# A decoder layer's seven-product weight pairs: an order of the units, the place of one weight sum, and two late additions

## The chip, the cores and the metric

The kernel runs as one program on one core of a Trainium2 chip. The metric is device time in microseconds, the median of several runs. A core has a matrix engine (TensorE, PE in the profile), VectorE (DVE), ScalarE (ACT), GpSimd (POOL) and SyncE (SP), each with its own in-order queue of instructions, and 16 DMA engines which they feed. Work of two engines is ordered only by semaphores: an instruction that waits holds back everything behind it on its engine.

## The reference

One decoder layer over 256 tokens of width 2048 in float32: retention and RG-LRU mixers side by side, a gated merge, cross-attention to 256 memory tokens, a convolutional gated FFN of width 5632, and a final norm. What matters here are three matrix products that end in a residual sum:

```
h = h + merged @ w_mix_out[l]
...
    return o @ w_o
...
    return (jax.nn.silu(gate) * val) @ w_down
```

## The kernel before

Almost all time goes into products with weights that are read once: `weight_plan` lists them, and `entry_units` (L117) cuts each into **units** of one megabyte, 4 blocks of 128 rows by 512 columns. Each unit is loaded to a tile `raw`, and then split in two float32r parts so that three fast products stand for one exact product: ScalarE rounds `raw` to `hi` (L281, "the cast"), VectorE makes `lo = raw - hi` (L282). TensorE then adds up activation-hi by weight-hi, activation-lo by weight-hi, and activation-hi by weight-lo.

`units` (L296) and `prefetch` (L241) run this as a stream. Ahead of the products of a unit, `prefetch` has written the load, the cast and the `lo` of the next two units (`AHEAD = 2`) into the program. There are five `raw` buffers, and three each for `hi` and `lo`: the cast of unit n takes the buffer of unit n-3, so it waits until TensorE is through with that unit. Loads are issued on SyncE in order, each waiting for a free `raw` buffer. `later(n, fn)` (L292) puts off a piece of work until n more units have been handed out. The order of instructions on each engine is in the end decided by a scheduler of the framework, which may pull single matmuls of a later unit ahead of the rest of an earlier one.

**Pairs.** Six times (once for `w_mix_out`, once for `xa_w_o`, and twice in each of the first two FFN parts) two neighbouring column blocks c0 and c1 of 512 are done together by `pair_add` (L364). Half of the contraction (k blocks 0 to 7) uses a seven-product scheme on 2x2 blocks: sums of the activations are made beforehand by `sums`, and sums of the weight blocks are made on the fly. The other half is done plainly. A pair is 11 units: seven "q" units of 12 matmuls each, and four "p" (plain) units of 24 matmuls. `PAIR_UNITS` (L98) is their order, written out by hand:

- q1 loads a block into a buffer that is kept, slot A. q3 loads a block into a second kept buffer, slot B.
- q2 is a plain load: column block c1 with the even k blocks; it multiplies plain activations.
- q5 uses A after a further block has been added to it. That addition is a DMA which accumulates (L260), issued on GpSimd. It must wait until the cast and the `lo` of q1 have read A.
- q6 uses A + B: `prefetch` makes that sum on VectorE (L262, 128 x 2048 elements) at the moment in which q6 is prepared, after q5's split has read A.
- q7 adds a block to B by accumulating DMA, after the sum has read B; q4 adds a block to A by accumulating DMA, after q6's split has read A.

The products of a pair go to three PSUM tiles of 128 x 1024: `xz` (halves x and z), `yv` (y and u), `rw` (r and w_). They are added to the two residual tiles h0 and h1 by VectorE (`add`, L383): x to h0 after q1, all of `rw` to h1 after q3, z twice to h1 after q5, x from h1 after q6, x to h0 and from h1 after q7, `yv` to h0 after q4. x is reused in between (q6 and q7 accumulate on), so q7's first product waits for q6's subtraction. In the program as built, 8 of the 24 matmuls of the third p stand ahead of q6's in all six pairs (the scheduler pulled them there), and in pairs 3 and 5 two of q5's stand near the beginning of the second p. Around the first pair, `memory_steps` has ScalarE square rows of `mem` (L882) between the casts.

Of the kernel before, what the change touches and what calls it, by code (L numbers as in the profile page):

```python
# [13 lines left out]
ALU = mybir.AluOpType  # L14
AX = mybir.AxisListType

P = 128
# [10 lines left out]
BW = 512  # L28
# [65 lines left out]
def residual_plan(w):  # L94
# [3 lines left out]
PAIR_UNITS = [  # L98
    ("q1", "A", ("new", 0, 0)),
    ("p", None, (1, 8)),  # L100
    ("q2", None, ("new", 1, 0)),
    ("p", None, (1, 12)),
    ("q3", "B", ("new", 1, 1)),
    ("q5", "A", ("add", 0, 1)),
    ("q6", "A", ("sum",)),
    ("p", None, (0, 8)),
    ("p", None, (0, 12)),
# [42 lines left out]
def hybrid_layer(  # L150
# [16 lines left out]
    act, dve, pe, pool, sp = nc.scalar, nc.vector, nc.tensor, nc.gpsimd, nc.sync  # L167
# [11 lines left out]
    def nm(s):  # L179
        count[0] += 1  # L180
        return f"{s}_{count[0]}"
# [7 lines left out]
    def acc():  # L189
        return pm.tile([P, 2, BW], F32, tag="acc", name=nm("acc"))  # L190
# [37 lines left out]
    held = {}  # L228
# [4 lines left out]
    def load_x(n):  # L233
        while len(xin) < n:
            t = big([P, 2, BW], s="nat")
            rows = x[0].rearrange("(t p) d -> p t d", p=P)
            c = len(xin) * BW
            act.dma_start(out=t, in_=rows[:, :, c : c + BW])
            xin.append(t)

    def prefetch(n):  # L241
        while len(ahead) < n and taken[0] < len(stream):
            kind, slot, op, i = stream[taken[0]]
            src = None if i is None else wall[i]
            taken[0] += 1
            first = taken[0] == 1
            if op == "new":
                raw = wp.tile([P, KC, BW], F32, tag="raw", bufs=RAW_BUFS, name=nm("raw"))
                if slot:
                    held[slot] = raw  # L250
            else:
                raw = held[slot]
            if taken[0] <= 4:
                xs.load(2 * taken[0] - 1)
            pieces = ((0, 1), (1, 2), (2, 4)) if first else ((0, 2), (2, 4)) if taken[0] <= 3 else ((0, 4),)
            for a, b in pieces:
                if op == "new":
                    sp.dma_start(out=raw[:, a:b, :], in_=src[:, a:b, :])
                elif op == "add":
                    pool.dma_start(out=raw, in_=src, accum_op=ALU.add)  # L260
                else:
                    dve.tensor_tensor(out=raw, in0=raw, in1=held["B"], op=ALU.add)  # L262
                if first and a == 0:
                    sp.dma_start(out=xs.rest[0], in_=xs.rest[1])
                elif first and a == 1 or a == 0 and taken[0] <= 4:
                    xs.load(2 * taken[0])
            if taken[0] == 5:
                sp.dma_start(out=cid, in_=consts[:, 0:C_DEC])
                sp.dma_start(out=pa[:, 16:P], in_=by_feature[:, 16:P])
                sp.dma_start(out=pb, in_=by_feature[:, P : P + 80])  # L270
            if taken[0] == 7:
                sp.dma_start(out=pf.rearrange("p a n -> p (a n)"), in_=by_feature[:, P + 80 :])
            hi = wp.tile([P, KC, BW], F32R, tag="hi", bufs=PART_BUFS, name=nm("hi"))
            lo = wp.tile([P, KC, BW], F32R, tag="lo", bufs=PART_BUFS, name=nm("lo"))
            for a, b in pieces:
                if taken[0] <= 4:
                    xs[2 * (taken[0] - 1) + (b - 1) // KH]
                if first and b <= KH:
                    dve.tensor_copy(hi[:, a:b], raw[:, a:b])  # L279
                else:  # L280
                    act.copy(hi[:, a:b], raw[:, a:b])  # L281
                dve.tensor_tensor(  # L282
                    out=lo[:, a:b], in0=raw[:, a:b], in1=hi[:, a:b].bitcast(F32), op=ALU.subtract
                )
            parts = [(hi[:, k : k + KH], lo[:, k : k + KH]) for k in range(0, KC, KH)]
            ahead.append((kind, parts))
            if taken[0] >= 4:
                load_x(min(4, 2 * (taken[0] - 3)))
# [3 lines left out]
    def later(n, fn):  # L292

        pending.append((step[0] + n + 1, fn))

    def units(*e):  # L296

        assert plan[gemms[0]] == e, (gemms[0], plan[gemms[0]], e)
        gemms[0] += 1
        for _ in entry_units(e):  # L300
            prefetch(1)
            kind, parts = ahead.pop(0)
            prefetch(AHEAD)
            yield kind, parts
            step[0] += 1
            due = [p for p in pending if p[0] <= step[0]]
            pending[:] = [p for p in pending if p[0] > step[0]]
            for _, fn in due:
                fn()
# [54 lines left out]
    def pair_add(w, row, st, ss, c0, c1, h0, h1):  # L364

        xz, yv, rw = acc(), acc(), acc()
        x, z, y, u, r, w_ = (t[:, i, :] for t in (xz, yv, rw) for i in range(2))
        where = {
            "q1": (x, "a", 0, 0), "q2": (y, "a", 1, 0), "q3": (r, "s", 3, 0), "q4": (u, "a", 1, 1),
            "q5": (z, "s", 0, 0), "q6": (x, "s", 1, 0), "q7": (x, "s", 2, 0),  # L370
        }
        begun, plain = set(), 0

        def run(o, key, ops, parts):
            for kk, (h, l) in enumerate(ops):
                hi, lo = (t[:, kk % KH, :] for t in parts[kk // KH])
                pe.matmul(o, h, hi, start=key not in begun, stop=False, skip_group_check=True)  # L377
                begun.add(key)
                pe.matmul(o, l, hi, start=False, stop=False, skip_group_check=True)  # L379
                pe.matmul(o, h, lo, start=False, stop=kk == KC - 1, skip_group_check=True)  # L380

        def add(o, i, op=ALU.add):
            dve.tensor_tensor(out=o, in0=o, in1=i, op=op)  # L383

        for kind, parts in units(w, row, NT, c0, c1):
            if kind == "p":
                k0, (a, b), (ka, kb) = ((8, (r, w_), "rw"), (12, (r, w_), "rw"), (8, (y, u), "yu"), (12, (y, u), "yu"))[plain]
                plain += 1
                for tt, (o, key) in enumerate(((a, ka), (b, kb))):
                    cs = slice(tt * P, (tt + 1) * P)  # L390
                    run(o, key, [halves(st[(k0 + k) // 2], k % 2, cs) for k in range(KC)], parts)
            else:
                o, t, j, tt = where[kind]
                if t == "a":
                    ops = [halves(st[k], j, slice(tt * P, (tt + 1) * P)) for k in range(KC)]
                else:
                    ops = [(ss[k][:, 0, j * P : (j + 1) * P], ss[k][:, 1, j * P : (j + 1) * P]) for k in range(KC)]
                key = {"q1": "x", "q4": "u", "q6": "x", "q7": "x", "q2": "y", "q3": "r", "q5": "z"}[kind]
                run(o, key, ops, parts)
            if kind == "q1":  # L400
                add(h0[:, 0, :], x)
            elif kind == "q3":
                add(h1, rw)
            elif kind == "q5":
                add(h1, z[:, None, :].to_broadcast([P, 2, BW]))
            elif kind == "q6":
                add(h1[:, 0, :], x, ALU.subtract)
            elif kind == "q7":
                add(h0[:, 1, :], x)
                add(h1[:, 1, :], x, ALU.subtract)  # L410
            elif kind == "q4":
                add(h0, yv)
# [27 lines left out]
    def halves(t, j, cs=slice(0, S)):  # L440

        return t[:, j, cs], t[:, j, S + cs.start : S + cs.stop]
# [12 lines left out]
    def joined(a, s="j"):  # L455

        c = tmp("c")
        o = tmp(s)
        with tc.high_priority(URGENT):
            act.copy(c, a[:, :, S:BW])  # L460
            dve.tensor_tensor(out=o, in0=a[:, :, 0:S], in1=c, op=ALU.add)  # L461
        return o
# [236 lines left out]
    for g in range(2):  # L699
        dec = big([P, 4, S], s="dec")  # L700
        vs, turned = [], []
        for b, o in enumerate((O_Q, O_K)):
            a = qjoin if g == b == 0 else [joined(t, "q") for t in gemm_t("w_in", 0, xs, NT, o + g * BW)]
            if b == 0:
                sp.dma_start(
                    out=dec,
# [245 lines left out]
    for b in range(XH):  # L952
        ks = []
        for a in gemm_t("xa_w_k", 0, ms, NT, b * BW):
            z = joined(a, "kz")
# [99 lines left out]
    for part, nb_ in enumerate(FF_PARTS):  # L1055
# [15 lines left out]
        if final:  # L1071
            wfin = []
            for i in range(2):
                t = big([P, 2, BW], s="wf")
                sp.dma_start(
                    out=t.rearrange("p a n -> p (a n)"),
# [3 lines left out]
        if nb_ == 4:  # L1080
            for b in (0, 2):
                pair_add("ffn_w_down", b0 * BW, hid, hid_sums, b * BW, (b + 1) * BW, hrow[b], hrow[b + 1])
        else:
            for b in range(4):
                down(b0, hid, b, final)
# [36 lines left out]
```

## Time and profile before

| what | value |
|---|---|
| median of 3 runs | 2067.07 us (2066.53 to 2070.82) |
| the profiled execution's own time | 2065.32 us |
| its span, first to last instruction | 2063.5 us |
| mean granted TensorE clock | 0.995 |
| HBM read | 401.04 MB, 195 GB/s over the span |
| starts of the six A + B sums (L262) | 852.4, 1237.2, 1512.1, 1556.3, 1781.5, 1825.7 us |

The profile page gives the busy time of each engine, the chain of work that ended last, and groups of instructions by source line. The trace behind it can be asked for a timeline of one engine, for the busy time and granted clock in chosen stretches ("windows"), for who waited for whom, and for the time from a DMA's issue to its landing. In a row of the timeline stand start, duration, engine, line, operation, tile written <- tiles read, and in brackets the idle time of the engine just before it with what ended that idle time. A matmul's duration there is its pipelined length; the distance of two starts is what counts. The six pairs lie at about 836 to 882, 1219 to 1267, 1493 to 1541, 1541 to 1585, 1763 to 1810 and 1811 to 1854 us. They are called pair 1 to pair 6 below. Pairs 3 and 4 follow each other without a gap, and so do 5 and 6.

### The profile page before, as it was taken

Reading aid. Unit: us, or ns where it says so; the run is one execution under the profiler, and the core shown is the slowest. Engines: PE = TensorE matmul, PEld = TensorE weight load, DVE = VectorE, ACT = ScalarE, POOL = GpSimd, SP = SyncE. Lnnn points to the kernel's source line nnn. Section 1 sums busy time; section 2 is a strip of 40 time slices with the busy share of each in tenths; the row PEclk is TensorE's granted clock in tenths of the full one; section 3 lists DMA queues with packets and bytes.
Section 4 is the critical chain, followed back from the end, with each engine's and each line's share of the span. In section 5 each row is a group of like instructions: output and inputs, shape, how many; then the busy total and the mean of one; then the engine's idle time right before and its main releaser. Section 6 shows DMA issues by size and latency. Waiting matters only on the chain.

```text
span 2063.5 us, 25096 instructions
## 1 busy us (share of the span) xinstructions
PE 2031.5 (98%) x10436; PEld 1735.4 (84%) x10436; DVE 1372.1 (66%) x1411; ACT 1039.6 (50%) x1042; POOL 23.7 (1%) x30
## 2 busy tenths in 40 slices
PE   9999999999999999999999999999999999999998
PEld 7888888888888888788888887888877888778887
DVE  6747658444688654666555656587786787776775
ACT  6445447433476544465444545555554555454543
POOL 0000000000000000000000000000000000000000
PEclk9999999999999999999999999999999999999999
DMA  9554553555553555865554447555567555675552
GB/s 371 208 206 163 184 194 143 204 186 202 198 199 143 201 187 184 265 238 211 182 184 164 163 163 224 184 188 183 193 194 263 186 190 195 183 245 204 185 203 82
DMA packets 66211, 404.76 MB, mean 196 GB/s; under 512 B 7217, under 2 KB 11953, under 8 KB 19377
## 3 DMA queue, kind: packets, MB, share of 16 engines
q1 hardware_dynamic: 61984, 381.66, 50.9%
q0 software_dynamic: 2592, 18.88, 4.9%
q10 hardware_dynamic: 1520, 2.63, 0.4%
q8 instruction: 81, 1.33, 0.2%
q14 instruction: 34, 0.27, 0.0%
HBM read 401.04 MB, written 2.10 MB: 195 GB/s over the span
## 4 chain that ended last, share of the span: by engine, by line
PE 91%; DVE 5%; ACT 2%; issue 1%; DMA 0%; SPq 0%; POOLq 0%; DVEq 0%; ACTq 0%
PE acc L339 43%; PE acc L349 12%; PE acc L351 12%; PE acc L350 12%; PE acc L380 3%; PE acc L377 3%; PE acc L379 3%; DVE lo L282 3%; PE sm L438 2%; ACT hi L281 1%; PE sm L450 1%; PE sm L764 0%; DVE raw L262 0%; DVE fv L998 0%; DMA raw<-in_wall 0%
## 5 line engine op out<-in xcount | busy, mean ns | idle before, releaser
L282 DVE TENSOR_TENSOR lo<-raw,hi 128x2048 fp32r<-128x2048 f32 (+2 forms) x378 | 855.8, 2267 | 531.2 <-ACT hi L281 530.7
L281 ACT CAST hi<-raw 128x2048 fp32r<-128x2048 f32 (+1 forms) x376 | 713.3, 1899 | 745.6 <-PE acc L350 291.9
L339 PE MATMUL acc<-s,hi 128*128 128x512 f32 x2688 | 638.8, 391 | 2.0 <-DVE hi L279 1.1
L339 PEld LDWEIGHTS acc<-s,hi 128*128 128x128 f32 x2688 | 496.4, 188 | 100.6 <-issue 2.2
L349 PE MATMUL acc<-hi,s 128*128 128x512 f32 (+1 forms) x1144 | 442.3, 387 | 0.0
L351 PE MATMUL acc<-lo,s 128*128 128x512 f32 (+1 forms) x1144 | 441.1, 386 | 0.0
L350 PE MATMUL acc<-hi,s 128*128 128x512 f32 (+1 forms) x1144 | 440.7, 385 | 0.0
L339 PEld LDWEIGHTS acc<-s,lo 128*128 128x128 f32 x2688 | 342.1, 191 | 12.7 <-DVE lo L282 1.9
L339 PE MATMUL acc<-s,lo 128*128 128x256 f32 x2688 | 349.6, 283 | 0.9 <-DVE lo L282 0.9
L351 PEld LDWEIGHTS acc<-lo,s 128*128 128x128 f32 x1144 | 215.0, 188 | 43.8 <-DVE lo L282 0.6
L349 PEld LDWEIGHTS acc<-hi,s 128*128 128x128 f32 x1144 | 215.1, 188 | 42.1 <-ACT s L471 0.3
L350 PEld LDWEIGHTS acc<-hi,s 128*128 128x128 f32 x1144 | 215.1, 188 | 41.9 <-DVE s L472 0.2
L380 PE MATMUL acc<-lo,s 128*128 128x512 f32 x264 | 105.5, 400 | 14.2 <-DVE lo L282 14.0
L377 PE MATMUL acc<-hi,s 128*128 128x512 f32 x264 | 105.1, 398 | 1.7 <-ACT hi L281 1.7
L379 PE MATMUL acc<-hi,s 128*128 128x512 f32 x264 | 105.1, 398 | 0.4 <-DVE s L472 0.4
L460 ACT COPY c<-acc 128x512 f32<-128x512 f32 x84 | 48.3, 579 | 99.1 <-PE acc L339 99.1
L380 PEld LDWEIGHTS acc<-lo,s 128*128 128x128 f32 x264 | 50.4, 191 | 27.8 <-DVE lo L282 17.7
L377 PEld LDWEIGHTS acc<-hi,s 128*128 128x128 f32 x264 | 50.6, 192 | 12.6 <-ACT hi L281 2.6
L379 PEld LDWEIGHTS acc<-hi,s 128*128 128x128 f32 x264 | 50.7, 192 | 11.9 <-DVE s L472 1.6
L383 DVE TENSOR_TENSOR nat<-nat,acc 128x512 f32<-128x512 f32 (+1 forms) x42 | 37.7, 910 | 20.0 <-PE acc L380 20.0
L461 DVE TENSOR_TENSOR uz<-acc,c 128x512 f32<-128x512 f32 x44 | 30.2, 686 | 20.2 <-ACT c L460 20.2
L377 PE MATMUL acc<-hi,ss 128*128 128x512 f32 x96 | 38.5, 401 | 1.9 <-ACT hi L281 1.9
(202 smaller groups left out, 1135.2 us busy)
## 6 DMA issues: line engine op xcount, KB each, us to landing
raw<-in_wall SPq DMA_DIRECT2D x347, 1024.0 KB, 4.8
raw<-in_wall POOLq DMA_DIRECT2D x18, 1024.0 KB, 8.6
raw<-in_wall SPq DMA_DIRECT2D x5, 512.0 KB, 7.2
nat<-in_x ACTq DMA_DIRECT2D x4, 512.0 KB, 11.3
nat<-in_x SPq DMA_DIRECT2D x4, 512.0 KB, 8.1
nat<-in_mem SPq DMA_DIRECT2D x4, 512.0 KB, 7.4
xt<-in_mem_t SPq DMA_DIRECT2D x8, 256.0 KB, 6.0
xt<-in_x_t SPq DMA_DIRECT2D x7, 256.0 KB, 7.5
```

The source lines that it names most:

```text
L281: act.copy(hi[:, a:b], raw[:, a:b])
L282: dve.tensor_tensor(out=lo[:, a:b], in0=raw[:, a:b], in1=hi[:, a:b].bitcast(F32), op=ALU.subtract)
L339: pe.matmul(a, part, sx, start=k == 0 and t == 0, stop=k == nk - 1 and t == 0, skip_group_check=True)
L349: pe.matmul(o, h, hi, start=start, stop=False)
L350: pe.matmul(o, l, hi, start=False, stop=False)
L351: pe.matmul(o, h, lo, start=False, stop=stop)
L377: pe.matmul(o, h, hi, start=key not in begun, stop=False, skip_group_check=True)
L379: pe.matmul(o, l, hi, start=False, stop=False, skip_group_check=True)
L380: pe.matmul(o, h, lo, start=False, stop=kk == KC - 1, skip_group_check=True)
L383: dve.tensor_tensor(out=o, in0=o, in1=i, op=op)
L438: pe.matmul(o, a, b, start=start and i == 0, stop=stop and i == 2, skip_group_check=True)
L460: act.copy(c, a[:, :, S:BW])
```

## The change

Three things are changed, all within a pair:

1. The order of units. Before: q1, p, q2, p, q3, q5, q6, p, p, q7, q4. Then: q1, p, q3, p, q5, q2, q6, p, p, q7, q4. The first p and the second p keep their data, and so does every q.
2. The sum A + B. It is now written right behind the split of q5, in the same call of `prefetch`, and no longer at the preparation of q6.
3. The additions of `rw` and of z to h1. They no longer come right after q3 and q5, but are put off by `later(2, ...)` and `later(3, ...)` from q5: they are handed in after q6 and after the plain unit behind it, 3 and 4 units on.

The amount of work is the same on every engine: as many matmuls, casts, subtractions, sums and loads of the same sizes. In the built program the PE order of pairs 1, 4 and 6 is now unit after unit. In pairs 3 and 5 the scheduler still pulls some matmuls ahead: two of q5 and two of q2 into the beginning of the second p, and two of the third p into q6. In pair 2 three matmuls of q5 stand within the second p. On VectorE the sum stands between the `lo` of q5 and that of q2 in pairs 1, 2, 4 and 6, and behind the `lo` of q2 in pairs 3 and 5. The additions of `rw` and z now stand between the `lo` of q7 and that of q4.

```diff
 PAIR_UNITS = [
     ("q1", "A", ("new", 0, 0)),
     ("p", None, (1, 8)),
+    ("q3", "B", ("new", 1, 1)),
+    ("p", None, (1, 12)),
+    ("q5", "A", ("add", 0, 1)),
     ("q2", None, ("new", 1, 0)),
-    ("p", None, (1, 12)),
-    ("q3", "B", ("new", 1, 1)),
-    ("q5", "A", ("add", 0, 1)),
     ("q6", "A", ("sum",)),
...
                 elif op == "add":
                     pool.dma_start(out=raw, in_=src, accum_op=ALU.add)
-                else:
-                    dve.tensor_tensor(out=raw, in0=raw, in1=held["B"], op=ALU.add)
...
+            if kind == "q5":
+                dve.tensor_tensor(out=raw, in0=raw, in1=held["B"], op=ALU.add)
             parts = [(hi[:, k : k + KH], lo[:, k : k + KH]) for k in range(0, KC, KH)]
...
-            elif kind == "q3":
-                add(h1, rw)
             elif kind == "q5":
-                add(h1, z[:, None, :].to_broadcast([P, 2, BW]))
+                later(2, lambda: add(h1, rw))
+                later(3, lambda: add(h1, z[:, None, :].to_broadcast([P, 2, BW])))
             elif kind == "q6":
                 add(h1[:, 0, :], x, ALU.subtract)
```

## The prediction

> **What bounds the kernel now.** I read the page first: busy time, then the chain that ended last, then the costliest groups.
>
> ```profile
> span 2063.5 us, 25096 instructions
> ...
> PE 2031.5 (98%) x10436; PEld 1735.4 (84%) x10436; DVE 1372.1 (66%) x1411; ACT 1039.6 (50%) x1042; POOL 23.7 (1%) x30
> ...
> PE 91%; DVE 5%; ACT 2%; issue 1%; DMA 0%; SPq 0%; POOLq 0%; DVEq 0%; ACTq 0%
> ...
> L282 DVE TENSOR_TENSOR lo<-raw,hi 128x2048 fp32r<-128x2048 f32 (+2 forms) x378 | 855.8, 2267 | 531.2 <-ACT hi L281 530.7
> L281 ACT CAST hi<-raw 128x2048 fp32r<-128x2048 f32 (+1 forms) x376 | 713.3, 1899 | 745.6 <-PE acc L350 291.9
> ```
>
> TensorE is the bound. No matmul goes away, so the change can give only what TensorE waits within the pairs. A unit needs 1.9 us of ScalarE (cast), then 2.27 us of VectorE (`lo`). The sum is as dear as a `lo`. Who TensorE waited for, in total, times, longest, and the row of the sum:
>
> ```profile
> PE acc L380 <- DVE lo L282: 14.0, 6, 2.5
> PE acc L377 <- ACT hi L281: 3.7, 5, 0.9
> ```
>
> ```profile
> L262 DVE TENSOR_TENSOR raw<-raw,raw x6: 2291/2292/2293, 852.4 to 1825.7; 128x2048 f32<-128x2048 f32 x6
> ```
>
> So there are six waits for a `lo`, one in each pair, each about 2.3 us. Next, stretches around them for pairs 1 to 6; columns: stretch, its length, PE busy (matmuls), granted clock, DMA share, GB/s.
>
> ```profile
> 858.00:866.00 8.00, 5.46 (x19) 0.79 1.00 202
> ...
> 1244.00:1252.00 8.00, 5.57 (x18) 0.79 0.99 207
> ...
> 1517.00:1525.00 8.00, 5.14 (x15) 0.79 0.92 189
> 1563.00:1567.00 4.00, 1.46 (x7) 1.00 1.02 203
> ...
> 1786.00:1794.00 8.00, 5.14 (x15) 0.79 1.02 191
> 1832.00:1836.00 4.00, 1.46 (x7) 1.00 1.08 215
> ```
>
> In pairs 1, 2, 3 and 5 the wait costs twice: 2.4 to 2.9 us idle, and then a lower clock: 0.21 of 8 us is 1.7 us, that is 3.4 us at half speed. Some of it falls into the wait itself; I count 1.5 us. In pairs 4 and 6 the same 2.5 us wait brought no drop. A wait costs 0.16 us more than the idle shown, because the last matmul before it is drawn 0.39 us long though the next could start after 0.227.
>
> The Trainium skill ("TensorE: Matmul & The Clock Gate", Part 1, What's actually happening) says that the clock falls to half after at least one idle window of about 3.4 us, and that this window runs freely. Read literally, no wait of 2.5 us would do it, and the drops would have another cause and would stay; the last rivals price that.
>
> What makes the wait in pair 1: PE, DVE and ACT timelines.
>
> ```profile
> 859.43 0.39 PE L379 MATMUL acc<-hi,s 128*128 128x512 f32 x1
> 862.36 0.79 PE L380 MATMUL acc<-lo,s 128*128 128x512 f32 x1 [2.54 <-DVE lo L282]
> ```
>
> ```profile
> 846.83 2.29 DVE L282 TENSOR_TENSOR lo<-raw,hi 128x2048 fp32r<-128x2048 f32 x1 [2.40 <-ACT hi L281]
> 849.04 0.68 DVE L472 SCALAR_TENSOR_TENSOR s<-sm,s 128x512 fp32r<-128x512 f32 x1
> ...
> 852.37 2.29 DVE L262 TENSOR_TENSOR raw<-raw,raw 128x2048 f32<-128x2048 f32 x1
> 856.69 1.22 DVE L383 TENSOR_TENSOR nat<-nat,acc 128x1024 f32<-128x1024 f32 x1 [2.02 <-PE acc L380]
> 857.83 4.49 DVE L282 TENSOR_TENSOR lo<-raw,hi 128x2048 fp32r<-128x2048 f32 x2
> ```
>
> ```profile
> 848.10 1.91 ACT L281 CAST hi<-raw 128x2048 fp32r<-128x2048 f32 x1 [0.81 <-PE acc L379]
> 853.30 0.63 ACT L882 ACTIVATE junk<-nat 128x512 f32<-128x512 f32 x1 [3.29 <-DMA nat<-in_mem]
> ...
> 854.77 3.71 ACT L281 CAST hi<-raw 128x2048 fp32r<-128x2048 f32 x2
> ```
>
> VectorE has done the sum at 854.7. Then it stands 2.0 us in front of the addition of `rw` to h1, which waits for q3's last product, and spends 1.2 us on it; only then come the two `lo` (q6, and the third p), done at 862.3. TensorE has wanted them since 859.7.
>
> **The change part by part.** Nothing is added or removed in work. DMA issues: SyncE's and GpSimd's loads are as many. With B held from the third unit on, some loads get a buffer later; in pair 1 that of the first unit behind the pair goes from 843 to about 854 (behind q2's `lo`), needed at 878, so nothing is lost.
>
> *Pair 1, with the new order.* A q unit is 12 x 0.227 = 2.72 us, a p unit 5.44. Until the third p (859.2 now) the mix of units is the same, so the second p ends at 853.8, q5 at 856.5, q2 at 859.2, q6 at 861.9. On VectorE: q5's `lo` takes the place of the row at 846.83 (same buffer, same release; A's added block has long landed), an activation split to 849.7, the sum to 852.0, q2's `lo` to 854.3; needed with q2's third matmul, 856.9. q6's cast: second p's end 853.8, behind two squares of `mem` 854.7, done 856.6; its `lo` 858.9; needed 859.7. Third p: cast behind two more squares 859.7, `lo` 862.0; needed 862.4. All in time, by 0.4 to 2.6 us. The additions to h1 come after the `lo` of q7, when their products have long been done: 2.4 us hidden beside the two long p units. The wait (862.36 - 859.43 - 0.23 = 2.7) and its half clock (1.5) go: **4.2**.
>
> *Pair 2* has the same rows with other neighbours; the same chain there leaves 0.8 us or more at each unit. Wait 2.6 (2.43 idle + 0.16) and clock 1.5: **4.1**. *Pairs 4 and 6*: the wait alone, **2.7** each.
>
> *Pairs 3 and 5* keep part of it, since the scheduler still interleaves. Pair 3 (5 is the same within 0.1 us):
>
> ```profile
> 1504.35 0.39 PE L377 MATMUL acc<-hi,s 128*128 128x512 f32 x1
> ...
> 1506.32 0.50 PE L377 MATMUL acc<-hi,ss 128*128 128x512 f32 x1 [0.88 <-ACT hi L281]
> ...
> 1507.14 0.50 PE L380 MATMUL acc<-lo,s 128*128 128x512 f32 x1
> ```
>
> ```profile
> 1518.27 0.50 PE L377 MATMUL acc<-hi,s 128*128 128x512 f32 x1 [0.87 <-ACT hi L281]
> ...
> 1521.00 0.79 PE L380 MATMUL acc<-lo,s 128*128 128x512 f32 x1 [1.99 <-DVE lo L282]
> ```
>
> ```profile
> 1530.26 0.39 PE L377 MATMUL acc<-hi,s 128*128 128x512 f32 x1
> ```
>
> ```profile
> 1507.61 4.49 DVE L282 TENSOR_TENSOR lo<-raw,hi 128x2048 fp32r<-128x2048 f32 x2
> 1512.12 2.29 DVE L262 TENSOR_TENSOR raw<-raw,raw 128x2048 f32<-128x2048 f32 x1
> ```
>
> ```profile
> 1514.51 5.51 ACT L281 CAST hi<-raw 128x2048 fp32r<-128x2048 f32 x3 [7.71 <-DVE raw L262]
> ...
> 1531.26 1.91 ACT L281 CAST hi<-raw 128x2048 fp32r<-128x2048 f32 x1 [2.74 <-DMA raw<-in_wall]
> ```
>
> The wait at 1506 stays (the cast of the sixth unit still needs the third unit's buffer), with two matmuls more done before it. From 1507.14 there follow 42 matmuls (22 of the second p, 10 of q5, 10 of q2) to 1516.7. q6's cast ends at 1516.4 as now; two of q6, then two of the third p, whose cast is the second of the row of three and ends at 1518.2: 1.15 us of waiting. q6's `lo` is no longer behind the h1 addition but starts with its cast's end all the same: 1518.7; third p's `lo` 1521.0. q6's other 10 matmuls end at 1521.1, the third p's other 22 at 1526.1. The fourth p starts then, at 1530.26 now: 4.2 won. A wait of 1.15 us is short of those that lowered the clock.
>
> Then a load is late. q4 needs A's second accumulated block, issued behind q6's `lo` as now:
>
> ```profile
> raw<-in_wall POOLq DMA_DIRECT2D x1, 1024.0 KB, 12.0
> ```
>
> It lands at 1531.2 (the row of the cast at 1531.26 shows who it waited for), so q4's `lo` is done about 1535.5; the new q4 would want it at 1534.7. At least 0.8 us come back; with a 1 MB load for the next pair now issued at 1512 instead of 1507 beside it, up to 2. I take 1.2, near the row. Net **3.0** each. The late `lo` pushes pair 4's (6's) second unit by an estimated 0.3, so those give **2.4**.
>
> Sum: 4.2 + 4.1 + 3.0 + 2.4 + 3.0 + 2.4 = 19.1 us. From the profiled run's 2065.3 us that is 2046.2; the median of the runs is 1.8 above that run, so **2048.0 us**.
>
> **The rivals.**
> - *The interleaving keeps all of pairs 3 and 5* (a wait moves to the cast that is pulled ahead, and lowers the clock again). For it: the 0.9 us cast waits at 1506.32 and 1518.27 stand before and after. Against it: no h1 addition stands there any more. Gain 4.2 + 4.1 + 2.4 + 2.4 = 13.1: 2054.0.
> - *The half clock stays*: stretches of 3.4 us are not the waits' doing. For it: the same wait left pairs 4 and 6 at 1.00. Against it: all four drops begin at such a wait. Gain 19.1 less 4 x 1.5: 2054.0. By the Trainium skill's rule above it would be this one; the 0.79 beside a 2.5 us wait speaks against the rule's size.
> - *The change doesn't do what it says*: margins of 0.4 to 0.8 us are eaten, and q2 or the third p waits behind the sum instead. Waits of some 2.5 us stay: 2063 to 2071.
> - *Slower: A's first accumulated block.* q5 now wants it one p unit earlier, and cast, `lo`, sum and q2's `lo` (1.9 + 2.3 + 2.3 + 2.3 = 8.8 us) hang behind it. In pairs 4 and 6 the issue comes with q1's `lo`, q2's third matmul 19.5 us later, so it must land within 10.3 us; in the others q1's `lo` is some 6 us ahead, so within 16. The 12.0 us row would cost 1.7 us there. At 18 us, pairs 4 and 6 wait 7.7 each and the others 1.7, with half clocks (1.5 each) 31 us: 2079. It decides from about 17 us on. For it: DMA share is 0.9 to 1.1 around the sums. Against it: 12.0 us was measured with two other loads beside it.
>
> **How the numbers follow.** Forecast 0.68; pairs 3 and 5 keep theirs 0.12; half clock stays 0.05; nothing gained 0.06; slower 0.09. About 0.2% (4 us) is what a measurement of this kernel can tell from no change. So faster 0.85, same 0.06, slower 0.09. Range: at the low end no late load and no 0.3 (3 us) and the first wait of pairs 3 and 5 gone too (2.6): 2042.5. At the high end pairs 3 and 5 unchanged, and one more half-clock stretch: 2056.
>
> **What would show it.** After the change: no L380 wait for a `lo` over 1 us in pairs 1, 2, 4, 6; windows of clock 1.00 there; no VectorE idle time in front of L383 that ends with a wait on q3; in pairs 3 and 5 waits of about 1.0 and 1.15 us for casts, and one of about 1 us at q4 whose cast waited for a DMA. Wrong it is if a wait over 2 us stands at q2, q6 or the third p, if the clock still drops, or if q5's cast waits for a DMA.

## The result and the profile after

The changed kernel took 2044.87 us (median of 4 runs, 2043.79 to 2046.83), the kernel before on the same chip 2066.8 (4 runs, 2064.23 to 2070.82): a ratio of 0.9893, 95% interval 0.9876 to 0.9911. That is 21.9 us won, where 19.1 were forecast, and inside the range. The span fell from 2063.5 to 2041.9 us, by 21.6.

The page of the profiled run after the change (span, busy time, chain, the two costliest groups of VectorE and ScalarE):

```profile
span 2041.9 us, 25079 instructions
...
PE 2026.0 (99%) x10436; PEld 1732.3 (85%) x10436; DVE 1371.0 (67%) x1411; ACT 1039.3 (51%) x1042; POOL 23.7 (1%) x30
...
PE 92%; DVE 4%; ACT 2%; DMA 1%; issue 1%; SPq 0%; POOL 0%; POOLq 0%; ACTq 0%; DVEq 0%
...
L280 DVE TENSOR_TENSOR lo<-raw,hi 128x2048 fp32r<-128x2048 f32 (+2 forms) x378 | 855.0, 2267 | 531.5 <-ACT hi L279 530.9
L279 ACT CAST hi<-raw 128x2048 fp32r<-128x2048 f32 (+1 forms) x376 | 712.8, 1899 | 725.0 <-PE acc L350 291.5
```

Each of these engines has as many instructions as before. What is gone is idle time and time at half clock (the latter makes TensorE's busy time fall from 2031.5 to 2026.0 us). TensorE's waits in the pairs (columns: total, times, longest):

```profile
PE acc L377 <- ACT hi L279: 3.2, 4, 0.9
...
PE acc L380 <- DVE lo L280: 0.2, 1, 0.2
```

The six waits for a `lo` (14.0 us before) have become one of 0.2. The windows around the q6 of pairs 1, 2 and 4, and around those of pair 3, where a wait was left (columns as in the prediction: length, PE busy, clock, DMA share, GB/s; busy PEld, DVE, ACT and POOL between):

```profile
856.00:864.00 8.00, 8.00 (x37) 6.60 (x36) 6.83 (x4) 6.85 (x8) 0.88 (x1) 1.00 1.05 274
1236.00:1244.00 8.00, 8.00 (x37) 6.61 (x36) 6.42 (x3) 5.58 (x4) 0.86 (x1) 1.00 0.91 244
1504.00:1512.00 8.00, 7.25 (x32) 5.57 (x31) 5.97 (x3) 5.52 (x3) 1.75 (x2) 1.00 0.86 218
...
1546.00:1554.00 8.00, 8.00 (x37) 6.61 (x36) 6.31 (x4) 5.38 (x3) 0.90 (x2) 1.00 0.91 214
```

In pairs 1, 2 and 4 TensorE is now busy for all of 8 us (5.46 and 5.57 in the windows of pairs 1 and 2 before), and the clock stays at 1.00 everywhere in the pairs. Pair 3 keeps 0.75 us of idle time in this window. Where the time came from: I add up, over the 512-wide matmuls, the distance of two starts beyond 0.227 us (distances over 0.300 only).

| stretch | before | after | won | forecast |
|---|---|---|---|---|
| pair 1 | 4.7 | 0.6 | 4.1 | 4.2 |
| pair 2 | 5.2 | 0.5 | 4.6 | 4.1 |
| pairs 3 and 4 | 9.6 | 3.2 | 6.4 | 5.4 |
| pairs 5 and 6 | 9.8 | 3.3 | 6.5 | 5.4 |

The sum of the third column, 21.6 us, is the whole difference of the spans. VectorE in pair 1, after:

```profile
850.13 2.28 DVE L284 TENSOR_TENSOR raw<-raw,raw 128x2048 f32<-128x2048 f32 x1
852.33 2.28 DVE L280 TENSOR_TENSOR lo<-raw,hi 128x2048 fp32r<-128x2048 f32 x1
856.21 2.29 DVE L280 TENSOR_TENSOR lo<-raw,hi 128x2048 fp32r<-128x2048 f32 x1 [1.60 <-ACT hi L279]
859.46 4.49 DVE L280 TENSOR_TENSOR lo<-raw,hi 128x2048 fp32r<-128x2048 f32 x2 [0.96 <-ACT hi L279]
863.87 0.68 DVE L383 TENSOR_TENSOR nat<-nat,acc 128x512 f32<-128x512 f32 x1
864.47 2.28 DVE L280 TENSOR_TENSOR lo<-raw,hi 128x2048 fp32r<-128x2048 f32 x1
866.67 2.47 DVE L383 TENSOR_TENSOR nat<-nat,acc 128x1024 f32<-128x1024 f32 x2
```

The sum ends at 852.4 (forecast 852.0), q2's `lo` at 854.6 (854.3), q6's at 858.5 (858.9), the third p's at about 861.7 (862.0); rw and z are added in one row of two at 866.67, behind q7's `lo`.

### The profile page after: what moved, and what is told of

It reads as the page before. It is cut to its first block, busy times and chain, and to the rows that moved or that the text cites. A ratio compares the mean times of both kernels' runs of the same rounds, so it can differ in the third digit from the quotient of the medians.

```text
span 2041.9 us, 25079 instructions
## 1 busy us (share of the span) xinstructions
PE 2026.0 (99%) x10436; PEld 1732.3 (85%) x10436; DVE 1371.0 (67%) x1411; ACT 1039.3 (51%) x1042; POOL 23.7 (1%) x30
## 4 chain that ended last, share of the span: by engine, by line
PE 92%; DVE 4%; ACT 2%; DMA 1%; issue 1%; SPq 0%; POOL 0%; POOLq 0%; ACTq 0%; DVEq 0%
PE acc L339 43%; PE acc L351 12%; PE acc L349 12%; PE acc L350 12%; PE acc L380 3%; PE acc L377 3%; PE acc L379 3%; PE sm L437 2%; DVE lo L280 2%; DMA raw<-in_wall 1%; ACT hi L279 1%; PE sm L449 1%; PE sm L763 0%; DVE fv L997 0%; DVE xr L780 0%
## 5 line engine op out<-in xcount | busy, mean ns | idle before, releaser
L997 DVE SCALAR_TENSOR_TENSOR fv<-uz,pf,fv 128x255 f32<-128x255 f32 (+1 forms) x88 | 39.6, 475 | 0.0
L997 DVE SCALAR_TENSOR_TENSOR fg<-uz,pf,fg 128x255 f32<-128x255 f32 (+1 forms) x88 | 38.2, 474 | 0.0
```

Source lines behind the costliest of these rows:

```text
L997: dve.scalar_tensor_tensor(out=y[:, s:S], in0=z[:, j, 0 : S - s], scalar=pf[:, 2 - s, t : t + 1], in1=y[:, s:S], op0=ALU.mult, op1=ALU.add,)
```

## Experiments: which part does it

The prediction named a cause (theory A): VectorE stands 2.0 us in front of rw's addition, and the splits behind it come late. A change of three parts lets one part carry the whole, so the late additions and the order were each tried alone, and the place of the sum was taken out of the change.

**The late additions alone.** Old order of units, old place of the sum:

```diff
-            elif kind == "q3":
-                add(h1, rw)
             elif kind == "q5":
-                add(h1, z[:, None, :].to_broadcast([P, 2, BW]))
+                later(1, lambda: add(h1, rw))
+                later(2, lambda: add(h1, z[:, None, :].to_broadcast([P, 2, BW])))
```

> The kernel before with its own unit order and its own place of the sum; only the additions of rw and z to h1 are put off (handed in after q6 and after the third p, as in the change). Theory A (VectorE stands in its queue in front of the addition of rw, which waits for q3's last product, and the splits behind it come late): the addition is out of the way, so the six waits for a lo of 2.3 to 2.5 us go, and the four stretches at half clock with them; 2045 to 2050 us. Theory B (the new unit order is what helps, since it brings q3 and q5 one unit earlier): the waits stay, 2062 to 2067 us.

Measured: 2043.94 us, ratio 0.9888 (0.9873 to 0.9903), the whole gain. The stretches with the old waits, of this kernel:

```profile
858.00:866.00 8.00, 8.00 (x37) 6.64 (x36) 6.86 (x5) 5.97 (x7) 0.87 (x1) 1.00 0.99 202
1244.00:1252.00 8.00, 8.00 (x37) 6.60 (x37) 6.16 (x5) 1.91 (x1) 0.00 (x0) 1.00 0.98 273
```

Theory B (only the order helps) falls.

**The new order alone.** `PAIR_UNITS` as in the change; the sum at q6's preparation; additions as early as they can be:

```diff
-            elif kind == "q3":
+            elif kind == "p" and plain == 2:
                 add(h1, rw)
             elif kind == "q5":
                 add(h1, z[:, None, :].to_broadcast([P, 2, BW]))
```

> The changed unit order alone: q1, p, q3, p, q5, q2, q6, p, p, q7, q4; the sum is handed in at the preparation of q6, and rw and z are added to h1 as soon as their last product is in the program (rw after the second p, z after q5). Theory A: the additions still stand in VectorE's queue ahead of the splits of q6 and of the third p, but what they wait for (the second p's end at about 853.8, q5's at about 856.5 us in pair 1) now comes before q6's cast is done (856.6), so VectorE loses 2.4 us of work and next to no standing; waits of 0 to 1 us a pair remain, no half clock: 2045 to 2051 us. Theory B: as the whole change, 2044 to 2046 us. If the late additions were the only thing that helps: near before, 2060 to 2067 us.

Measured: 2045.9 us, ratio 0.9896 (0.9881 to 0.9910). The order alone brings the whole gain too. So the two parts are two cures for one ailment, and they don't add. What ailment, a small new wait of this kernel tells (its waits, then TensorE in pair 4):

```profile
PE acc L377 <- DVE nat L383: 1.8, 3, 0.8
```

```profile
1555.08 0.47 PE L377 MATMUL acc<-hi,ss 128*128 128x512 f32 x1 [0.83 <-DVE nat L383]
```

q6's first product waits for an *addition to h1*. (In the rows, `ss` are the summed activations, which q3, q5, q6 and q7 use, and `s` the plain ones; q6 writes to x.) I had priced the additions only as time on VectorE, not as something that TensorE waits for.

**The sum's place.** The change with the sum made at the preparation of q6 again:

```diff
                 elif op == "add":
                     pool.dma_start(out=raw, in_=src, accum_op=ALU.add)
+                else:
+                    dve.tensor_tensor(out=raw, in0=raw, in1=held["B"], op=ALU.add)
...
-            if kind == "q5":
-                dve.tensor_tensor(out=raw, in0=raw, in1=held["B"], op=ALU.add)
```

> The change with the sum A + B handed in at the preparation of q6 again, as before; new unit order and late additions are kept. Theories A and B: the same as the change, 2043.5 to 2047 us, since VectorE is told the sum in the same place among its instructions. Theory C (it is the earlier sum that frees q6): a wait of 2 us or more comes back in each pair, 2056 to 2067 us.

Measured: 2045.02 us, ratio 0.9889 (0.9874 to 0.9903). The written place of the sum is worth nothing here: the scheduler puts it in the same place of VectorE's queue either way (in pair 1 behind the `lo` of q5 and ahead of that of q2, at 850.13 us in the change and at 851.33 in this kernel). In the old order no run shows the place of the sum by itself.

**Each addition alone.** Old order; only rw's addition put off, z's right behind q5, and then the other way round:

```diff
-            elif kind == "q3":
-                add(h1, rw)
             elif kind == "q5":
+                later(1, lambda: add(h1, rw))
                 add(h1, z[:, None, :].to_broadcast([P, 2, BW]))
```

> The kernel before with only the addition of rw put off (handed in after q6); z is still added right behind q5, order of units and sum as before. Theory A (it is rw's addition that VectorE stands in front of): nearly all of the gain, 2044 to 2048 us, no wait for a lo over 1 us in pairs 1, 2, 4 and 6. Rival (both additions must go): a third to a half of it, 2052 to 2060 us.

```diff
             elif kind == "q3":
                 add(h1, rw)
             elif kind == "q5":
-                add(h1, z[:, None, :].to_broadcast([P, 2, BW]))
+                later(2, lambda: add(h1, z[:, None, :].to_broadcast([P, 2, BW])))
```

> The kernel before with only the addition of z put off (handed in after the third p); rw is still added right behind q3. Theory A: rw's addition stands in the same place, right behind the sum in pairs 1, 3 and 5 and elsewhere ahead of the third p's lo as before, so the waits stay at 2 us or more: 2061 to 2067 us. Rival (it is z's addition, or the sum of both, that counts): 2044 to 2056 us.

Measured, and it is the opposite of what theory A says: rw alone 2058.62 us, ratio 0.9961 (0.9946 to 0.9976), 8 us won; z alone 2046.75 us, ratio 0.9905 (0.9889 to 0.9922), some 20. **Theory A falls.** With rw put off, TensorE still waits:

```profile
PE acc L380 <- DVE lo L282: 10.1, 6, 2.0
```

and pair 1 says why the 2 us of standing did not go (kernel with only rw late, VectorE, then ScalarE):

```profile
853.14 2.29 DVE L262 TENSOR_TENSOR raw<-raw,raw 128x2048 f32<-128x2048 f32 x1
857.49 4.49 DVE L282 TENSOR_TENSOR lo<-raw,hi 128x2048 fp32r<-128x2048 f32 x2 [2.05 <-PE acc L380]
861.90 1.21 DVE L383 TENSOR_TENSOR nat<-nat,acc 128x1024 f32<-128x1024 f32 x1
```

```profile
855.54 3.72 ACT L281 CAST hi<-raw 128x2048 fp32r<-128x2048 f32 x2 [0.69 <-DVE raw L262]
```

Without the addition, VectorE stands just as long in front of q6's `lo`, since q6's cast must come between the sum (done 855.4) and the `lo`: 1.9 us from 855.54. (The row names a product of TensorE as releaser; the one whose buffer this `lo` takes, the second p's last, was over by 854.8, so it was the cast.) Only about the time of the addition itself was won, 0.9 to 1.1 us in each of four pairs, and two of the four half clocks; pairs 3 and 5 kept their waits. With z put off instead, VectorE stands 2.06 us in front of rw's addition as ever, and TensorE doesn't mind (VectorE, then TensorE; kernel with only z late):

```profile
856.77 1.22 DVE L383 TENSOR_TENSOR nat<-nat,acc 128x1024 f32<-128x1024 f32 x1 [2.06 <-PE acc L380]
857.91 6.69 DVE L282 TENSOR_TENSOR lo<-raw,hi 128x2048 fp32r<-128x2048 f32 x3
```

```profile
859.29 0.39 PE L377 MATMUL acc<-hi,ss 128*128 128x512 f32 x1
...
859.75 0.39 PE L377 MATMUL acc<-hi,s 128*128 128x512 f32 x1
859.97 0.39 PE L379 MATMUL acc<-hi,s 128*128 128x512 f32 x1
860.25 0.50 PE L380 MATMUL acc<-lo,ss 128*128 128x512 f32 x1
```

q6 (`ss`) starts right behind q5, with two products of the third p behind its first two; its `lo` comes 0.05 us late, and the third p's `lo` (done at about 862.4) is wanted only at 862.67. In the kernel before, with VectorE's rows the same up to there, this came instead (VectorE, then TensorE, pair 1 of before):

```profile
862.23 1.21 DVE L383 TENSOR_TENSOR nat<-nat,acc 128x1024 f32<-128x1024 f32 x1
```

```profile
864.66 0.63 PE L379 MATMUL acc<-hi,s 128*128 128x512 f32 x1
865.09 0.48 PE L377 MATMUL acc<-hi,ss 128*128 128x512 f32 x1
```

z's addition was done at 863.4, and q6's first product began behind it, at 865.09. That it waits for just that addition is read from the built program; in this trace the wait was over by then. So the scheduler had put eight products of the third p ahead of q6, and these needed the third p's `lo` (862.3) from 859.66 on. That gives **theory H**: x and z are the two halves of one PSUM tile; a product written to x must wait until an addition that reads z, and that the program hands in ahead of it, is through; with that addition behind two `lo` on VectorE, q6 can't be next, though its own `lo` is there at 860.1, and TensorE waits for the wrong unit's.

**Theory H by itself.** The kernel before in all, but with other halves sharing a tile, so that q6 doesn't share with z:

```diff
-        xz, yv, rw = acc(), acc(), acc()
-        x, z, y, u, r, w_ = (t[:, i, :] for t in (xz, yv, rw) for i in range(2))
+        xw, zu, yr = acc(), acc(), acc()
+        x, w_, z, u, y, r = (t[:, i, :] for t in (xw, zu, yr) for i in range(2))
...
-                add(h1, rw)
+                add(h1[:, 0, :], r)
+                add(h1[:, 1, :], w_)
...
-                add(h0, yv)
+                add(h0[:, 0, :], y)
+                add(h0[:, 1, :], u)
```

> The kernel before in its old order, with the sum and both additions where they were, but with other neighbours in the PSUM tiles: x with w_, z with u, y with r, in place of x with z, y with u, r with w_ (rw and yv are then added by two 128x512 additions each, about 0.15 us more per pair and tile). So q6, which writes x, no longer has to wait until z has been added to h1. On VectorE rw's addition still stands right behind the sum in pairs 1 and 2, ahead of q6's lo. Theory H (formed after the runs with one late addition each: the loss of before comes from q6's products waiting for z's addition, so that the third p goes ahead of q6 and its lo is wanted 2.7 us too early): nearly all of the gain, 2045 to 2050 us, waits for a lo of at most 1 us. Theory A (VectorE's standing in front of rw's addition): the waits of 2 us and more stay, 2061 to 2068 us.

Measured: 2052.88 us, before 2066.02 to 2072.38 with a median of 2070.66 in this comparison; ratio 0.9921 (0.9901 to 0.9941), about 16 us won: less than forecast, far from theory A's 0. VectorE and TensorE in pair 1 of this kernel:

```profile
857.32 0.69 DVE L383 TENSOR_TENSOR nat<-nat,acc 128x512 f32<-128x512 f32 x1 [0.38 <-PE acc L380]
858.39 4.50 DVE L282 TENSOR_TENSOR lo<-raw,hi 128x2048 fp32r<-128x2048 f32 x2 [0.39 <-ACT hi L281]
862.81 1.22 DVE L383 TENSOR_TENSOR nat<-nat,acc 128x1024 f32<-128x1024 f32 x1
```

```profile
860.74 0.50 PE L380 MATMUL acc<-lo,ss 128*128 128x512 f32 x1
```

rw's two additions stand ahead of both `lo`, z's behind them, in the old order; and q6 now runs while z is still unread. The wait of 2.5 us in pairs 1 and 2 is gone; what is left of pairs 1 and 2 by the measure of the table is 0.7 and 0.2 us (4.7 and 5.2 before). Most of the missing 6 us is the same rule at another place, where I had made new neighbours: the first p writes w_ beside x, and in pairs 3 and 5 its first product to w_ waits 1.95 us for the addition of x to h0. One stretch of half clock, from 1765.17 us, follows the second of these. New as well are waits of 1.6 and 1.1 us for a `lo` right behind pairs 1 and 2; what makes them stays open.

```profile
PE acc L377 <- DVE nat L383: 4.6, 4, 2.0
```

```profile
1499.44 0.50 PE L377 MATMUL acc<-hi,s 128*128 128x512 f32 x1 [1.95 <-DVE nat L383]
```

So sharing is shown twice: undone it takes the wait away, made anew it makes one.

**Another order of the plain units.** For the waits left in pairs 3 and 5, the change with its second and third plain unit swapped (the table of what each plain unit multiplies is swapped with them, and the two additions are put off by one unit more):

```diff
-    ("p", None, (1, 12)),
+    ("p", None, (0, 8)),
     ("q5", "A", ("add", 0, 1)),
     ("q2", None, ("new", 1, 0)),
     ("q6", "A", ("sum",)),
-    ("p", None, (0, 8)),
+    ("p", None, (1, 12)),
...
```

> The change with its second and third plain unit swapped: k blocks 8 to 11 of the other side now second, k blocks 12 to 15 of the first side third, which only the last activations of an FFN block feed; rw is then complete one plain unit later, and its addition and z's are put off one unit further. If the scheduler pulls units apart in pairs 3 and 5 because the second p needs the FFN block's last activations (theory D): the waits for a cast there (1.0 us at the second p, 0.9 us at the third p, twice) go or move, 2041 to 2043.5 us. If the pulling apart has another cause (rival): within 1 us of the change, 2044 to 2046 us. Slower than the change by 1 us or more if the third p, now with the late activations, waits instead.

Measured: 2044.33 us, ratio 0.9891 (0.9874 to 0.9907), no gain over the change. The waits only changed their names:

```profile
PE acc L380 <- DVE lo L280: 4.7, 4, 1.7
...
PE acc L377 <- ACT hi L279: 0.5, 2, 0.3
```

The casts' 3.2 us became 4.7 us for `lo`s (1.7 us at the second p of pairs 3 and 5, 1.05 in pair 4) and 0.5 for casts. Theory D is not borne out; what makes the 3 us left in each of pairs 3 and 5 stays open.

**What lowers the clock.** The kernel before, once more, and the change with halves of the third p's `lo` made again (dose 2, 3, 4, 3 in pairs 1, 2, 4, 6):

```diff
...
+                for i in range((0, 2, 3, 0, 4, 0, 3)[pairs] if seen == 3 else 0):
+                    a = KH * (i % 2)
+                    dve.tensor_tensor(
+                        out=lo[:, a : a + KH], in0=raw[:, a : a + KH], in1=hi[:, a : a + KH].bitcast(F32), op=ALU.subtract
+                    )
```

> The kernel before, unchanged, profiled once more. Clock theory F (the grid of 3.41 us runs freely against the program): the six waits are the same 2.3 to 2.5 us, but the pairs in which the clock falls need not be 1, 2, 3 and 5 this time; the time moves by 1.5 us for each stretch more or fewer: 2061 to 2069 us. Rival (the pair decides, for instance by what else runs beside it): again pairs 1, 2, 3 and 5, and 2065 us.

> The change with work added to VectorE: in pairs 1, 2, 4 and 6 halves of the third p's lo are made again (2, 3, 4 and 3 times 128x1024, 1.2 us each; same values into the same place, so nothing else changes). The late additions left VectorE a margin here: in pair 1 the third p's lo is done at 861.7 and wanted at 862.9 us. Theory A (only VectorE's time ahead of a lo counts, beyond its margin): pair 1 waits about 2.4 - 1.1 = 1.3 us, pairs 2 and 6 about 3.6 less 1.1 to 1.6 = 2.0 to 2.5, pair 4 about 4.8 less 1.1 to 1.6 = 3.2 to 3.7; 9 us in all. Clock theory F (a wait lowers the clock when over about 2.2 us of TensorE idling fall into one of the stretches of 3.41 us on which the clock is set): none in pair 1, in pairs 2 and 6 as the grid falls, in pair 4 likely, so 1 to 3 stretches at half clock, 1.5 us each: 2054 to 2059 us. Rival G (some 3.4 us of idling are needed): none in pairs 1, 2 and 6, 2053 to 2054.5 us, and then the half clock of before had another cause.

Measured: 2067.55 us for before, 2057.78 for the repeats (one run each). In the new run of before the six waits are the same 14.0 us, but a fifth stretch of half clock has come, in pair 6. The window of 3.41 us around pair 6's wait and the one behind it, in the first run (full clock) and in the second:

```profile
1831.24:1834.65 3.41, 1.73 (x8) 1.11 (x6) 3.41 (x2) 2.51 (x2) 0.86 (x1) 1.00 0.96 197
1834.65:1838.06 3.41, 2.54 (x11) 2.13 (x12) 3.41 (x3) 0.00 (x0) 0.00 (x0) 1.00 1.04 197
```

```profile
1832.26:1835.68 3.42, 1.43 (x7) 0.85 (x5) 3.42 (x2) 2.20 (x2) 0.86 (x1) 1.00 0.99 204
1835.68:1839.09 3.41, 2.86 (x7) 2.28 (x8) 3.41 (x3) 0.00 (x0) 0.00 (x0) 0.50 1.04 199
```

The wait had not changed; it fell otherwise on the grid. With the repeats, TensorE waited only for the half of `lo` that it reads first: next to nothing in pair 1, and 1.95 to 2.06 us in pairs 2, 4 and 6 (distance of starts less 0.227), so the doses of 3 and 4 gave the same wait, and my 3.2 to 3.7 for pair 4 was wrong. The time of this run holds more than the repeats: q7's first product in pair 1 waited 1.05 us for q6's subtraction, and in pair 3, which has no repeats, A's second accumulated block, issued at 1515.48, kept its cast waiting until 1529.18, so that q4 waited and one of the three half clocks (from 1534.29) came there:

```profile
1533.46 0.50 PE L393 MATMUL acc<-lo,s 128*128 128x512 f32 x1 [1.59 <-DVE lo L283]
```

So the total says little between the theories; the windows decide. For the clock the equal waits are the better test. Pairs 4 and 6 have the same wait of 1.95 us:

```profile
1561.60:1565.01 3.41, 1.62 (x8) 1.04 (x7) 3.41 (x4) 1.90 (x1) 0.00 (x0) 1.00 1.09 283
1565.01:1568.43 3.42, 3.42 (x10) 2.64 (x9) 3.42 (x4) 0.00 (x0) 0.00 (x0) 0.50 0.96 204
1827.84:1831.25 3.41, 1.81 (x8) 1.15 (x7) 3.38 (x4) 0.36 (x1) 0.00 (x0) 1.00 1.03 298
1831.25:1834.67 3.42, 3.23 (x14) 2.70 (x15) 3.42 (x4) 1.91 (x1) 0.00 (x0) 1.00 1.03 264
```

One lowered the clock and the other didn't. Rival G (3.4 us of idling are needed) falls; theory F holds with its limit a little lower than I put it, as the last section tells.

## Why the prediction was right, and where its reason was wrong

The time was right, and so was nearly every landing that the working listed; the cause that it gave for the old wait was not.

- **"What makes the wait in pair 1"**: the rows were read rightly (`lo` of the third p done at 862.3, wanted from 859.7), but the step "VectorE stands 2.0 us in front of the addition of rw ... only then come the two `lo`" took the first idle gap on VectorE for the cause. Without rw's addition the standing stays (2.05 us, for q6's cast) and so does most of the wait; it isn't even lost time, as the kernel with only z late has it and doesn't wait. I did not ask why TensorE wanted the third p's `lo` at 859.7 at all, with q6 next in the written order and its `lo` done at 860.1. I had noted the eight products pulled ahead as a given of the scheduler; they were the symptom. The wait ahead of them was q6's, on z's addition. The forecast held because the change removes that in both ways: q2 now stands between q5 and q6, and z's addition is handed in behind q6. The landings of the new order were worked out soundly, whatever had made the old wait; that the change also takes away the cause that the working had not seen was luck.
- **Pairs 1 and 2**: 4.2 and 4.1 forecast, 4.1 and 4.6 measured. The half clock went with the waits, as said.
- **Pairs 3 and 5**: the two waits left for casts were forecast at about 1.0 and 1.15 us, and are there (distances of starts less 0.227: 1.05 and 0.91 in pair 3; idle time in brackets):

```profile
1498.03 0.50 PE L377 MATMUL acc<-hi,s 128*128 128x512 f32 x1 [0.88 <-ACT hi L279]
...
1509.85 0.50 PE L377 MATMUL acc<-hi,s 128*128 128x512 f32 x1 [0.75 <-ACT hi L279]
...
1526.72 0.50 PE L380 MATMUL acc<-lo,s 128*128 128x512 f32 x1 [0.19 <-DVE lo L280]
```

- **The late load at q4** was the mis-sized term: 1.2 us forecast, 0.35 in pair 3 (last row) and 0.18 in pair 5. The load was about as slow as forecast: issued at 1510.73, and the cast that waited for it began at 1522.43, 11.7 us later (12.0 in the row that I used). The issue came where the working had it, 0.88 us behind the third p's first product at 1509.85 (about 0.85 in the forecast). Of the 1.2 us, 0.8 came from the rows; the rest was an allowance for the load beside it, which this run did not need. The term is not steady, though: in the run with the repeats the same load took 13.7 us in pair 3, and q4 waited 1.59 us.

```profile
1510.73 0.87 POOL L260 DMA_DIRECT2D raw<-in_wall  x1 [3.19 <-DVE lo L280]
```

```profile
1522.43 5.52 ACT L279 CAST hi<-raw 128x2048 fp32r<-128x2048 f32 x3 [5.30 <-DMA raw<-in_wall]
```

- **Pairs 4 and 6**: the 0.3 us handed on from that load did not show apart. With the late load, that was 3.0 us of the forecast and about 0.5 as measured, which covers the 2.1 us by which pairs 3 to 6 gave more than forecast.
- **The rivals**: no pair kept its wait for a `lo` of 2 us, and no half clock stayed. The slower case did not come, but its first bound was near. In pairs 4 and 6 q5's cast did wait for A's first accumulated block, which the prediction had listed as a sign of being wrong; here the row of pair 4:

```profile
1537.95 1.91 ACT L279 CAST hi<-raw 128x2048 fp32r<-128x2048 f32 x1 [4.23 <-DMA raw<-in_wall]
```

TensorE did not wait, so the sign was too strict. The load had been issued at 1529.27 in pair 4 and landed 8.6 us later; in pair 6 it took 9.6, and q2's `lo` was done there 1.0 us before TensorE wanted it. So at about 10.6 us TensorE would have begun to wait in this run. That is what the working should have given too (19.5 less 8.8 is 10.7; it has 10.3), and the run with the order alone had 10.1 at this place. The page's median for the 18 accumulating loads, 1 MB each, is 9.2 us, 8.6 before.

## What to carry to other kernels

When an engine idles, ask first why it is at that instruction and not at the next one that is ready: an instruction that a scheduler has pulled ahead often marks another that may not start. Two halves of one PSUM tile are tied together by this program's waits, so what TensorE writes next should not share a tile with what another engine has yet to read; give them other neighbours, a unit between them, or hand the read in later. And try the parts of a change one by one before believing the reason for it, since two of three here did the same thing and the third did nothing.

## What the runs showed of the hardware

The clock is set window by window, on a grid of 3.413 us that lies otherwise against the program in each run: in the first run of before it falls at 861.85 and 1247.56 us, 385.71 apart, which is 113 times 3.413. The six traces with such a drop (before twice, rw late, repeats, order alone, other tiles) hold, the end of the program left out, 16 windows at half clock that follow one at full clock. In the full window ahead, TensorE was busy for 0.73 to 1.63 of 3.41 us. Every window with 1.51 us or less was followed by half clock (14 of them), none with 1.73 us or more; of three between 1.57 and 1.63, two were. (In the five other traces the least busy full window had 1.69 us, and none was followed by half clock, again but for the end.) So an idle share of a little over half a window is enough in these traces, and a wait of 2 us can cost 3.5, or 2, by where it falls. The Trainium skill ("TensorE: Matmul & The Clock Gate", Part 1, What's actually happening) gives the window (3413 ns, free-running), and the traces agree. It also lets the clock fall after at least one idle window of that length; if idle means without any work, the traces contradict that, since TensorE was busy for up to 1.63 us of the window ahead.

The wait of q6 for z is one of the program. The Trainium skill ("PSUM — Partial Sum Buffer", PSUM bank collisions raise a hardware error) says that two engines may work side by side in different banks; by its bank size of 2 KB a partition, x and z (512 floats each) would lie in two. No run here has q6 write x while z is being read, so whether the chip needs the wait stays open.
